# Hybrid decoder step: the norm row spread on TensorE, and two chunks put ahead of the sample

## The chip, the cores and the metric

One core of a Trainium2 chip runs the kernel. The metric is device microseconds of one execution, as the median of three runs. TensorE is PE, VectorE DVE, ScalarE ACT, GpSimd POOL, and SP the engine that does nothing but issue DMAs. Each engine works its own list of instructions strictly in order, and waits at the head of the list.

## The reference

The kernel is one inference step of two layers, a retention layer and a sliding-window attention layer, on 1024 prompt tokens and, with the same weights, on 8 sample tokens. All of it is float32, with 1024 features per token. What matters here is how the retention layer begins.

```python
def rmsnorm(x, g):
    xf = x.astype(jnp.float32)
    y = xf * lax.rsqrt(jnp.mean(xf * xf, axis=-1, keepdims=True) + EPS)
    return (y * g.astype(jnp.float32)).astype(x.dtype)

def retention_layer(x, S0, g_norm, w_in, g_out, w_out):
    h = rmsnorm(x, g_norm)
    proj = h @ w_in
    q, k, v, gate = jnp.split(proj, [RET_QK, 2 * RET_QK, 2 * RET_QK + RET_V], axis=-1)
    ...
    o, S = retention_scan(q, k, v, S0)
    ...
    return x + o @ w_out, S.astype(S0.dtype)
```

`g_norm` is one row of 1024 numbers, the norm row. The retention scan that follows the projections runs over chunks of 128 tokens and four heads.

## The kernel before

**Precision and products.** Every operand of a large product is split in two parts, a rounded one (`xh`, `woh`; `hi`, `w_hi`, on ACT) and the residual (`xl`, `wol`; `lo` on DVE, `w_lo` on POOL or DVE). A product is then three passes on PE: hi by hi, hi by lo, lo by hi. The weights of one head's q (set `q0`) come as four blocks A11, A12, A21, A22 of a 2x2 split, and the activations as blocks B11, B21 and so on.

**Chunks.** The prompt comes in as chunks c = 0 to 7 of 128 tokens (`X[c]`; tiles `xq`, `u`, one of `raw`) and the sample as c = 8, with 8 rows (a tile `u`). Each passes the same helpers: `xload` (SP issues its DMA), `sq` (ACT, L431: square and row sum), `pw` (POOL, L435 and L120: two small steps, the inverse root), `sc` (DVE, L440: scale the rows and multiply by `gb`), `TR` (PE, L105: eight transposes into two PSUM banks), `hi` (ACT, L457) and `lo` (DVE, L461). Their cores read:

```python
def sc(c):
    n = X[c].shape[0]
    dve.scalar_tensor_tensor(X[c], X[c], SS[c][:n], gb[:n], MUL, MUL)
def TR(c, b):
    PO[c] = [bank(b, j).rearrange("p (k t) -> p k t", k=4) for j in range(2)]
    for j in range(2):
        for k in range(4):
            tr(PO[c][j][:, k, :], X[c][:, 512 * j + k * 128:512 * j + k * 128 + 128], ident)
```

`gb` holds the norm row in all 128 partitions; a DMA writes it from the row, 512 KB in all. The sample takes another way after `sc`: eight transposes of 8 rows into a PSUM tile `pd8`, a copy into `rdec`, and `dcols` (DVE, L495 and L496), which writes two of its columns, rounded and as residual, behind the 256 prompt columns of B11 and B21. A first product of 258 columns (`plain`, L544) therefore needs chunks 0 and 2 and the sample, and A11 and A12.

**Order.** The order of an engine's list is the order in which the Python code calls the helpers. A hand-written opening takes chunks 8, 0 and 2 up to the first product; after it a table `ops` interleaves the helpers of the other chunks with the 16 first products, the next being chunk 1 (its transposes stand on PE behind two products).

**DMA semaphores.** All DMAs of SP and ACT take eight semaphores DMAHW0 to DMAHW7 in turn, and a DMA waits until the one that used its semaphore before has landed. So the semaphore that a DMA's row names in its wait is as a rule the one it raises itself.

**The ring of raw tiles and the memory under it.** `raw_tile()` (tag `raw`, five buffers of 4 KB per partition) hands out buffers in turn: first the raw weights of q0 and k0, then chunk 7, then all further weights. The last set of projections uses four of these tiles for its results as well; POOL scales them (L393) and SP spills them to DRAM, in eight DMAs `gsc<-raw` (L397). When the projections end, the pool is closed, and the scan's pools `rp0` and `rp` are laid over the same memory, with `reuse_waits="tile"`: the first writer of a new tile waits for whoever still uses the old tile under it.

```python
return wq.tile([128, 1024], F32, tag="raw", bufs=5, name="raw")
...
r = (raw_tile()[:, 0:516] if s is sets[-1] else ring(key)).rearrange("p (t n) -> p t n", t=2)
...
nc.sync.dma_start(out=M23, in_=a["c1"][:, 384:640])
```

In the scan a step loads q and k (`evp<-qks`, L735), v (`evx<-vsc`, L742) and the gate (`evc` or `evw<-gsc`, L748) on SP. DVE masks the scores (`sT`, L796), scales the finished output (`on`, L1067) and makes k's residual (`kl`, L791); ACT rounds the state (`Sh`, L1037) and `sT` (`sTh`, L801); PE transposes `on` (L105). M23, loaded at L1552, holds the masks of heads 2 and 3.

Of the kernel before, what the change touches and what calls it, by code (L numbers as in the profile page):

```python
# [7 lines left out]
F32 = mybir.dt.float32  # L8
# [6 lines left out]
D = 1024  # L15
# [45 lines left out]
def trunk(tc, x_prompt, x_sample, state_ret, cache_k, cache_v, norm_ret, w_in_ret, ret_out_norm,  # L61
          w_out_ret, norm_swa, w_in_swa, q_norm, k_norm, sinks, w_out_swa, c1, c2,
          y_p, y_s, nrp, nrs, nkp, nvp, nks, nvs):
    nc = tc.nc
    ctx = ExitStack()
    with ctx:
        ctx.enter_context(tc.manual_schedule(engines=MS))
        _trunk(ctx, tc, nc, locals())


def _trunk(ctx, tc, nc, a):
    x_prompt, x_sample, state_ret = a["x_prompt"], a["x_sample"], a["state_ret"]
    cache_k, cache_v = a["cache_k"], a["cache_v"]
    norm_ret, ret_out_norm, norm_swa = a["norm_ret"], a["ret_out_norm"], a["norm_swa"]
# [22 lines left out]
    mm = nc.tensor.matmul  # L97
# [6 lines left out]
    def tr(out, in_, ident, start=True, stop=True):  # L104
        nc.tensor.matmul(out, in_, ident, is_transpose=True, start=start, stop=stop)  # L105
# [13 lines left out]
    def rsq(out, in_, n):  # L119
        nc.gpsimd.tensor_tensor(out, in_, mhalf[:in_.shape[0], :n], ALU.pow)  # L120
# [13 lines left out]
    dcp = sa.enter_context(tc.tile_pool(name="dcp", bufs=1, reuse_waits="tile"))  # L134
    wq = sa.enter_context(tc.tile_pool(name="wq", bufs=1, reuse_waits="tile"))
# [26 lines left out]
    def bank(i, t):  # L162
        return abp.tile([128, 512], F32, tag=f"b{i}{t}", name=f"b{i}{t}")
# [7 lines left out]
    act, dve, pool = nc.scalar.activation, nc.vector, nc.gpsimd  # L171
# [21 lines left out]
    def src_of(s, name, sub):  # L193
        if name[0] == "A":
            return quad(s, int(name[1]) - 1, int(name[2]) - 1, sub)
        return s.sum[name, sub]
# [16 lines left out]
    def w_hi(s, name, sub):  # L213
        sh = [128, 512 // s.fw, s.fw]

        if (s.kind, s.h) == ("q", 0) and name in ("A11", "A12"):
            tag, n = ("s1", 2) if name == "A11" else ("s2", 2)
        else:
            tag, n = "wop", 12
        s.op[name, sub] = [wq.tile(sh, F32R, tag=tag, bufs=n, name=nm) for nm in ("woh", "wol")]  # L220
        act(s.op[name, sub][0], src_of(s, name, sub), AF.Copy)  # L221

    def w_lo(s, name, sub, eng=None):
        hi, lo = s.op[name, sub]
        eng = eng or (pool if name in ("A12", "A22") else dve)
        eng.tensor_tensor(lo, src_of(s, name, sub), hi.bitcast(F32), SUB)  # L226
# [183 lines left out]
    gb = sp.tile([128, D], F32, name="gb")  # L410
# [6 lines left out]
    def xload(c):  # L417
        if c in (0, 1, 2, 3):
            X[c] = xq.tile([128, D], F32, tag="xq", bufs=4, name="xq")
        elif c == 7:  # L420
            X[c] = raw_tile()
        else:
            X[c] = sp.tile([128, D], F32, tag="u", bufs=3, name="u")
        if c == 8:
            X[c] = X[c][0:ND, :]
        nc.sync.dma_start(out=X[c], in_=x_sample[:, 0, :] if c == 8 else x_prompt[0, c * 128:c * 128 + 128, :])

    def sq(c):
        SS[c] = sp.tile([128, 1], F32, name="ss", bufs=4)
        n = X[c].shape[0]  # L430
        act(junk[:n], X[c], AF.Square, accum_out=SS[c][:n])  # L431

    def pw(c):
        n = X[c].shape[0]
        pool.tensor_scalar(SS[c][:n], SS[c][:n], 1.0 / D, EPS, MUL, ADD)  # L435
        rsq(SS[c][:n], SS[c][:n], 1)
# [11 lines that stand above are left out]
# [4 lines left out]
    def where(c, j):  # L452
        return c // 4, ((B11, B21), (T3, B22))[c % 2][j], slice(128 * (c // 2 % 2), 128 * (c // 2 % 2) + 128)

    def hi(c, j):
        t, x, cs = where(c, j)
        act(XH[t][x][:, :, cs], PO[c][j], AF.Copy)  # L457

    def lo(c, j):
        t, x, cs = where(c, j)  # L460
        dve.tensor_tensor(XL[t][x][:, :, cs], PO[c][j], XH[t][x].bitcast(F32)[:, :, cs], SUB)  # L461
# [27 lines left out]
    def dcols(t, x, src=None):  # L489

        if src is None:
            k0, r0 = DB[x]
            src = rdec[:, k0:k0 + 4, r0 + 2 * t:r0 + 2 * t + 2]
        h = XH[t][x][:, :, 256:258]
        dve.tensor_copy(h, src)  # L495
        dve.tensor_tensor(XL[t][x][:, :, 256:258], src, h.bitcast(F32), SUB)  # L496
# [95 lines left out]
    q0, k0 = sets[0], sets[1]  # L592
# [270 lines left out]
    for r in range(2):  # L863
        pool.memset(oneh[:, r, r:r + 1], 1.0)
    pool.memset(rdec32, 0.0)
    nc.scalar.dma_start(out=gb, in_=norm_ret[0].partition_broadcast(128))
    nc.scalar.dma_start(out=ident, in_=a["c1"][:, 0:128])
    act(warm, warm, AF.Silu)
    for c in (0, 8, 2):
        xload(c)  # L870
# [5 lines left out]
        raw_load(k0, r, nc.sync)  # L876
    for c in (4, 6, 7):
        xload(c)
    for c in (8, 0, 2):
        sq(c)  # L880
        pw(c)
    sc(8)
    p8 = vdp.tile([128, 8, ND], F32, tag="vd", name="pd8")
    for k in range(8):
        tr(p8[:, k, :], X[8][:, k * 128:k * 128 + 128], ident[:ND, :ND])
    sc(0)
    TR(0, 1)
    dve.tensor_copy(rdec, p8)
    sc(2)
    TR(2, 2)  # L890
    dcols(0, B11)
    dcols(0, B21)
    for c, name in ((0, "A11"), (2, "A12")):
        for j in range(2):
            hi(c, j)
            lo(c, j)
        w_hi(q0, name, 0)
        w_lo(q0, name, 0, pool)
    ev.sort(key=lambda e: e[:2])
    for n, s in enumerate(slots):  # L900
        while pes and pes[0][0] <= s.t:
# [1348 lines left out]
    out = so_all()  # L2250
# [159 lines left out]
```

## Time and profile before

| | |
|---|---|
| median of three runs | 1292.86 us (1292.46 to 1294.36) |
| the profiled execution | 1292.86 us |
| its span, first to last instruction | 1291.0 us |
| mean granted TensorE clock | 0.997 |
| busy: PE, PEld, POOL, DVE, ACT | 98%, 94%, 55%, 60%, 51% |
| DMA, mean over the span | 160 GB/s |
| start of the first product | 15.76 us |

In the rows shown, the first number is the start in microseconds from the span's start, the second the duration; then the engine, the line, the operation and out<-in; xN is a count. In brackets stands the idle time of the engine just before, and what ended it. q1 is SP's DMA queue and q10 that of ACT; a row of a queue gives packets, megabytes and the share of the 16 DMA engines in the stretch asked for. A row of `windows` gives, after the stretch and its length, the busy time of PE, PEld, DVE, ACT and POOL with counts, the granted clock, the DMA share and GB/s.

### The profile page before, as it was taken

What the parts mean: (1) busy time and instruction counts of PE and PEld (TensorE: products, weight loads), DVE (VectorE), ACT (ScalarE), POOL (GpSimd) and SP (SyncE); (2) the same over time, 40 slices, a digit from 0 to 9 for tenths busy, and PEclk for the clock granted to TensorE, in tenths of its full rate; (3) what the DMA queues carried; (4) which work ended last, traced back from release to release, by engine and by line L of the source; (5) the groups of instructions that cost most, each with busy time, mean ns of one, the idle gap of its engine ahead of it and who ended that gap; (6) DMA issues with size and microseconds to landing.
All of it is one profiled execution on the core that took longest, in us unless ns stands there. A gap on an engine that the chain in (4) does not pass through costs nothing.

```text
span 1291.0 us, 26757 instructions
## 1 busy us (share of the span) xinstructions
PE 1266.2 (98%) x9839; PEld 1214.3 (94%) x9839; DVE 778.1 (60%) x1506; ACT 656.9 (51%) x1592; POOL 711.8 (55%) x822
## 2 busy tenths in 40 slices
PE   6999999999999999999999999999999999998998
PEld 5999999999999999888889999999999999998998
DVE  5954646665575764476774656764667766775421
ACT  5533445454555554578771235545566656663121
POOL 5654444535359899788771457726475655432000
PEclk9999999999999999999999999999999999998999
DMA  6313867687678673556879955843031222137232
GB/s 227 108 54 121 253 183 231 183 253 219 186 210 226 192 240 107 180 174 200 261 211 247 251 187 161 272 120 103 20 112 50 66 67 67 66 101 245 74 98 79
DMA packets 221967, 206.68 MB, mean 160 GB/s; under 512 B 32729, under 2 KB 196821, under 8 KB 221821
## 3 DMA queue, kind: packets, MB, share of 16 engines
q1 hardware_dynamic: 189840, 170.61, 44.2%
q10 hardware_dynamic: 31996, 34.36, 8.2%
q8 instruction: 78, 1.28, 0.4%
q14 instruction: 53, 0.43, 0.1%
HBM read 135.41 MB, written 70.55 MB: 160 GB/s over the span
## 4 chain that ended last, share of the span: by engine, by line
PE 90%; DVE 3%; DMA 2%; ACT 1%; POOL 1%; issue 1%; SPq 0%; ACTq 0%; POOLq 0%; DVEq 0%
PE S L1302 9%; PE b L335 8%; PE b L336 8%; PE b L337 8%; PE pj L1661 6%; PE pj L1662 5%; PE pj L1663 5%; PE b L328 4%; PE tr L105 4%; PE b L329 4%; PE b L330 4%; PE o L2023 2%; PE b L544 1%; PE S L335 1%; PE S L336 1%; PE S L337 1%
## 5 line engine op out<-in xcount | busy, mean ns | idle before, releaser
L335 PE MATMUL b<-xh,woh 128*128 128x258 f32 x784 | 223.2, 285 | 0.0
L337 PE MATMUL b<-xh,wol 128*128 128x258 f32 x784 | 221.7, 283 | 0.0
L336 PE MATMUL b<-xl,woh 128*128 128x258 f32 x784 | 221.6, 283 | 0.0
L1661 PE MATMUL pj<-SA,wh 128*128 128x384 f32 (+1 forms) x496 | 169.3, 341 | 4.5 <-ACT SA L2045 3.7
L1662 PE MATMUL pj<-SA,wh 128*128 128x384 f32 (+1 forms) x496 | 159.5, 322 | 0.7 <-DVE SA L2046 0.7
L1663 PE MATMUL pj<-SA,wl 128*128 128x384 f32 (+1 forms) x496 | 159.4, 321 | 0.0
L335 PEld LDWEIGHTS b<-xh,woh 128*128 128x128 f32 x784 | 148.0, 189 | 4.1 <-issue 3.7
L336 PEld LDWEIGHTS b<-xl,woh 128*128 128x128 f32 x784 | 148.7, 190 | 0.0
L337 PEld LDWEIGHTS b<-xh,wol 128*128 128x128 f32 x784 | 148.0, 189 | 0.0
L226 POOL TENSOR_TENSOR wol<-raw,woh 128x512 fp32r<-128x512 f32 x51 | 66.1, 1303 | 120.3 <-ACT woh L221 118.2
L328 PE MATMUL b<-woh,xh 128*128 128x256 f32 x448 | 126.6, 283 | 0.0
L329 PE MATMUL b<-wol,xh 128*128 128x256 f32 x448 | 126.0, 281 | 0.0
L330 PE MATMUL b<-woh,xl 128*128 128x256 f32 x448 | 125.6, 280 | 0.0
L2001 POOL TENSOR_TENSOR s<-s,sm 128x512 f32<-128x512 f32 x64 | 67.1, 1048 | 87.4 <-DVE sm L2000 76.4
L1661 PEld LDWEIGHTS pj<-SA,wh 128*128 128x128 f32 x496 | 93.9, 189 | 8.4 <-ACT SA L2045 4.0
L1662 PEld LDWEIGHTS pj<-SA,wh 128*128 128x128 f32 x496 | 94.3, 190 | 0.9 <-DVE SA L2046 0.9
L1663 PEld LDWEIGHTS pj<-SA,wl 128*128 128x128 f32 x496 | 93.9, 189 | 0.0
L1993 ACT ACTIVATE s<-s,mx 128x257 f32<-128x257 f32 x128 | 64.2, 503 | 48.9 <-DVE mx L1991 45.8
L328 PEld LDWEIGHTS b<-woh,xh 128*128 128x128 f32 x448 | 84.3, 188 | 5.0 <-issue 2.9
L330 PEld LDWEIGHTS b<-woh,xl 128*128 128x128 f32 x448 | 84.3, 188 | 0.0
L329 PEld LDWEIGHTS b<-wol,xh 128*128 128x128 f32 x448 | 84.3, 188 | 0.0
L221 ACT ACTIVATE woh<-s 128x512 fp32r<-128x512 f32 x88 | 54.1, 624 | 54.1 <-POOL s L211 20.7
(529 smaller groups left out, 3586.9 us busy)
## 6 DMA issues: line engine op xcount, KB each, us to landing
raw<-in_w_in_ret_dram ACTq DMA_DIRECT2D x44, 512.0 KB
st<-in_state_ret_dram SPq DMA_DIRECT2D x64, 256.0 KB
out_dram<-st SPq DMA_DIRECT2D x64, 256.0 KB
vb<-vscr SPq DMA_DIRECT2D x64, 128.0 KB
evp<-qks SPq DMA_DIRECT2D x32, 256.0 KB
evx<-vsc SPq DMA_DIRECT2D x32, 256.0 KB
wr<-in_w_in_swa_dram SPq DMA_DIRECT2D x32, 256.0 KB
evc<-gsc SPq DMA_DIRECT2D x16, 256.0 KB
```

The costliest lines, as they stand in the source:

```text
L226: eng.tensor_tensor(lo, src_of(s, name, sub), hi.bitcast(F32), SUB)
L328: mm(dst, xh, wh, start=a and i == 0, stop=False, skip_group_check=True)
L329: mm(dst, xh, wl, start=False, stop=False, skip_group_check=True)
L330: mm(dst, xl, wh, start=False, stop=z, skip_group_check=True)
L335: mm(dst, wh, xh, start=a, stop=False, **sg)
L336: mm(dst, wh, xl, start=False, stop=False, **sg)
L337: mm(dst, wl, xh, start=False, stop=z, **sg)
L1302: mm(box[0], s.op[f"A{i + 1}{j + 1}", 0][w][:, k, :], xs_[t][x[j]][:, k, :], start=(xs_ is XH and w == 0 and j + k == 0), stop=(xs_ is XL ...
L1661: mm(ps, hi[:, k, fs], xh[:, k, t0:t1], start=first and k == ks[0], stop=False)
L1662: mm(ps, hi[:, k, fs], xl[:, k, t0:t1], start=False, stop=False)
L1663: mm(ps, lo[:, k, fs], xh[:, k, t0:t1], start=False, stop=last and k == ks[-1])
L2001: nc.gpsimd.tensor_tensor(st[:, :, 0:256], st[:, :, 0:256], sm.unsqueeze(2).broadcast_to([128, 2, 256]), ALU.mult)
```

## The change

The norm row is loaded as one row of 4 KB, into a tile of the raw ring (`grow`). Two products of a row of ones (`row1`) with its halves spread it over the 128 partitions in PSUM, in the banks that the first product uses later, and two DVE copies bring it to `gb`. On every engine chunks 0 and 2 now come ahead of the sample, and DVE takes chunk 0's residuals before the sample's columns.

```diff
-    nc.scalar.dma_start(out=gb, in_=norm_ret[0].partition_broadcast(128))
+    grow = wq.tile([1, D], F32, tag="raw", bufs=5, name="raw")
+    nc.scalar.dma_start(out=grow, in_=norm_ret[0:1, :])
     nc.scalar.dma_start(out=ident, in_=a["c1"][:, 0:128])
+    row1 = dcp.tile([1, 128], F32, name="row1")
+    dve.memset(row1, 1.0)
     act(warm, warm, AF.Silu)
     for c in (0, 8, 2):
         xload(c)
     ...
     for c in (4, 6, 7):
         xload(c)
-    for c in (8, 0, 2):
+    bank_of = {}
+    for j in range(2):
+        bank_of[0, j] = bank(0, j)
+        mm(bank_of[0, j], row1, grow[:, 512 * j:512 * j + 512], start=True, stop=True)
+    for j in range(2):
+        dve.tensor_copy(gb[:, 512 * j:512 * j + 512], bank_of[0, j])
+    for c in (0, 2, 8):
         sq(c)
         pw(c)
+    sc(0)
+    TR(0, 1)
+    sc(2)
+    TR(2, 2)
     sc(8)
     p8 = vdp.tile([128, 8, ND], F32, tag="vd", name="pd8")
     for k in range(8):
         tr(p8[:, k, :], X[8][:, k * 128:k * 128 + 128], ident[:ND, :ND])
-    sc(0)
-    TR(0, 1)
+    for j in range(2):
+        hi(0, j)
+        lo(0, j)
+    w_hi(q0, "A11", 0)
+    for j in range(2):
+        hi(2, j)
     dve.tensor_copy(rdec, p8)
-    sc(2)
-    TR(2, 2)
     dcols(0, B11)
     dcols(0, B21)
-    for c, name in ((0, "A11"), (2, "A12")):
-        for j in range(2):
-            hi(c, j)
-            lo(c, j)
-        w_hi(q0, name, 0)
-        w_lo(q0, name, 0, pool)
+    for j in range(2):
+        lo(2, j)
+    w_lo(q0, "A11", 0, pool)
+    w_hi(q0, "A12", 0)
+    w_lo(q0, "A12", 0, pool)
```

DVE at the program's start, before; `b_184`, `b_185` are chunk 0's PSUM tiles, `b_196`, `b_197` chunk 2's, `pd_174` the sample's:

```order
L861 MEMSET warm 1x8
L440 SCALAR_TENSOR_TENSOR u<-u,ss,gb 8x1024
L440 SCALAR_TENSOR_TENSOR xq<-xq,ss,gb 128x1024
L888 COPY rdec<-pd_174 128x8x8
L440 SCALAR_TENSOR_TENSOR xq<-xq,ss,gb 128x1024
L495 CAST xh<-rdec 128x4x2
L496 TENSOR_TENSOR xl<-rdec,xh 128x4x2
L495 CAST xh<-rdec 128x4x2
L496 TENSOR_TENSOR xl<-rdec,xh 128x4x2
L461 TENSOR_TENSOR xl<-b_184,xh 128x4x128
```

The same place now; `b_164`, `b_166` hold the spread row, `b_183`, `b_184` are chunk 0's:

```order
L870 MEMSET row_137 1x128
L887 COPY gb<-b_164 128x512
L887 COPY gb<-b_166 128x512
L440 SCALAR_TENSOR_TENSOR xq<-xq,ss,gb 128x1024 x2
L440 SCALAR_TENSOR_TENSOR u<-u,ss,gb 8x1024
L461 TENSOR_TENSOR xl<-b_183,xh 128x4x128
L461 TENSOR_TENSOR xl<-b_184,xh 128x4x128
L905 COPY rdec<-pd_205 128x8x8
L495 CAST xh<-rdec 128x4x2
L496 TENSOR_TENSOR xl<-rdec,xh 128x4x2
```

The memset and two copies are new, the sample's scale (`u`) has gone behind both chunks', and its copy and casts behind chunk 0's residuals.

Further on, near 541 us, where the scan's tiles are first used, the order of the rows is the same as before, and their waits are not. SP, before, from the last three spills on:

```order
L397 DMA gsc<-raw 128x2x128 [waits DMAHW5_49,Pool_49]
L397 DMA gsc<-raw 128x2x128 [waits DMAHW6_49,Pool_49]
L397 DMA gsc<-raw 128x2x128 [waits DMAHW7_49,Pool_49]
L1552 DMA M_7448<-const_c_dram 128x256 [waits DMAHW0_49]
L742 DMA evx<-vsc 128x512 [waits DMAHW1_49,Activation_49]
```

The last two of these five now:

```order
L1566 DMA M_7457<-const_c_dram 128x256 [waits DMAHW5_49,DMAHW1_49,DMAHW0_49]
L742 DMA evx<-vsc 128x512 [waits Activation_49]
```

M23's load has gained the waits for DMAHW5 and DMAHW1, the first of the last three spills and the one before it, which are the two halves of one raw tile.

DVE there, before (`sT`, `on` and `kl` of one step):

```order
L796 TENSOR_TENSOR sT<-tr,M_89 128x128 [waits DMAHW1_49,PE_49]
L1067 TENSOR_SCALAR on<-po,ss 128x512 [waits Pool_49]
L791 SCALAR_TENSOR_TENSOR kl<-tr,M_89,kh 128x256 [waits Activation_49]
```

And now:

```order
L796 TENSOR_TENSOR sT<-tr,M_89 128x128 [waits DMAHW6_49,DMAHW7_49,PE_49,Pool_49]
L1081 TENSOR_SCALAR on<-po,ss 128x512 [waits PE_49,Pool_49]
L791 SCALAR_TENSOR_TENSOR kl<-tr,M_89,kh 128x256 [waits Activation_49]
```

`sT` waited for a weight load of long before (DMAHW1) and now waits for the second and third of the last three spills. On ACT the opposite happened: `Sh` waited for DMAHW1, DMAHW5 and two older spills, and now for one older spill (DMAHW0) alone, while `sTh` ahead of it waits, as `sT` does, for DMAHW6 and DMAHW7.

## The prediction

> **What bounds the kernel now.** I read the page's busy times and chain first, then the first 25 us instruction by instruction, then the DMA queues there, then the place near 541 us where the built program's waits differ.
>
> ```profile
> PE 1266.2 (98%) x9839; PEld 1214.3 (94%) x9839; DVE 778.1 (60%) x1506; ACT 656.9 (51%) x1592; POOL 711.8 (55%) x822
> PE 90%; DVE 3%; DMA 2%; ACT 1%; POOL 1%; issue 1%; SPq 0%; ACTq 0%; POOLq 0%; DVEq 0%
> ```
>
> PE is busy for 98% of the span and carries 90% of the chain: a microsecond is won only where PE waits. The change touches a time when PE has nothing to do yet. Timeline of that start (start, us, engine, line):
>
> ```profile
> 6.51 1.06 ACT L431 ACTIVATE junk<-u 8x1024 f32<-8x1024 f32 x1 [3.35 <-DMA u<-in_x_sample_dram]
> 7.69 1.06 ACT L431 ACTIVATE junk<-xq 128x1024 f32<-128x1024 f32 x1
> 8.60 1.27 DVE L440 SCALAR_TENSOR_TENSOR u<-u,ss,gb 8x1024 f32<-8x1024 f32 x1 [7.69 <-POOL ss L120]
> 8.93 1.00 POOL L435 TENSOR_SCALAR ss<-ss 128x1 f32<-128x1 f32 x1 [0.36 <-ACT junk L431]
> 9.92 1.01 PE L105 MATMUL pd<-ident,u 8*128 8x8 f32 x8 [9.92 <-DVE u L440]
> 10.01 0.56 POOL L120 TENSOR_TENSOR ss<-ss,mhalf 128x1 f32<-128x1 f32 x1
> 10.61 1.28 DVE L440 SCALAR_TENSOR_TENSOR xq<-xq,ss,gb 128x1024 f32<-128x1024 f32 x1 [0.74 <-POOL ss L120]
> 11.95 3.65 PE L105 MATMUL b<-ident,xq 128*128 128x128 f32 x16 [1.01 <-DVE xq L440]
> 12.62 1.28 DVE L440 SCALAR_TENSOR_TENSOR xq<-xq,ss,gb 128x1024 f32<-128x1024 f32 x1 [0.59 <-POOL ss L120]
> 14.39 2.65 DVE L461 TENSOR_TENSOR xl<-b,xh 128x512 fp32r<-128x512 f32 x4
> 15.76 0.75 PE L544 MATMUL b<-xh,woh 128*128 128x258 f32 x4 [0.17 <-ACT xh L457]
> 16.13 1.66 ACT L221 ACTIVATE woh<-raw 128x512 fp32r<-128x512 f32 x3
> 16.83 3.80 POOL L226 TENSOR_TENSOR wol<-raw,woh 128x512 fp32r<-128x512 f32 x3 [0.40 <-ACT woh L221]
> 20.98 0.54 POOL L120 TENSOR_TENSOR ss<-ss,mhalf 128x1 f32<-128x1 f32 x1
> 21.55 2.30 DVE L440 SCALAR_TENSOR_TENSOR xq<-xq,ss,gb 128x1024 f32<-128x1024 f32 x1 [3.33 <-POOL ss L120]
> 24.00 1.06 PE L105 MATMUL b<-ident,xq 128*128 128x128 f32 x8 [1.21 <-DVE xq L440]
> ```
>
> The chain to follow: sample landed (6.51), its square, scale and transposes; chunk 0 behind it (scale 10.61), chunk 2 (12.62), A12 rounded (16.13), three POOL residuals (16.83), chunk 1's scale (21.55), chunk 1's transposes on PE (24.00). From 24.00 on PE is nearly gapless, so what the change is worth at the start is how much earlier that last row comes.
>
> **The norm row.** The 512 KB broadcast goes, a 4 KB row comes. In the first rows of two DMA windows (2 to 2.5 us, and 2.5 to 5 us) and in SP's waits, q1 is SP's queue, q10 ACT's:
>
> ```profile
> q10 hardware_dynamic: 8, 0.03, 42.8%
> q1 hardware_dynamic: 101, 0.41, 50.9%
> q10 hardware_dynamic: 96, 0.39, 50.2%
> SPq L426 <- DMA gb<-in_norm_ret_dram: 2.5, 1, 2.5
> ```
>
> While chunk 0 comes in, the broadcast takes half of the engines. Alone, the same 0.41 MB of q1 take half of the 2.5 us. The sample, behind chunk 0 on that queue, then lands near 5.2 instead of 6.5; chunk 0, ahead of it, and with the shared stretch past 5.0 not counted yet, I put at 4.7 (range 4.4 to 5.4). Every later SP load comes about 1.3 us sooner; chunk 2, half a megabyte behind at the 0.8 MB that both queues moved in 2.5 us, at 6.2. SP's wait of 2.5 us for the broadcast's semaphore goes too; behind it stood chunk 3 and the next weights, while the loads issued before were streaming anyway.
>
> No row shows a 4 KB load at the start. ACT's first packets move between 2.0 and 2.5, so it cannot land before 2.4; later than chunk 0 at 4.7 it would be only if it were served behind it. I take 3.1, nearer the first, since nothing stands ahead of it on its queue.
>
> Two products of 1x128 by 1x512 are added on PE. The nearest row is the plain fp32 product of 512 columns:
>
> ```profile
> 76.76 1.92 PE L344 MATMUL vd<-raw,rdec 128*32 128x512 f32 x16
> L344 PE MATMUL vd<-raw,rdec 128*32 128x512 f32 x64 | 7.7, 598 | 0.0
> 26.82 1.13 PE L544 MATMUL b<-xl,woh 128*128 128x258 f32 x8
> L465 DVE COPY xq<-b 128x512 f32<-128x512 f32 x4 | 2.6, 680 | 0.0
> ```
>
> One lasts 0.60 us. The transposes at 11.95 take 3.65 for 16, at 24.00 1.06 for 8, half the pace, though the granted clock reads 1.00 in both windows; so early products cost double, some 1.0 us, and one starts 0.85 after the other. Products 3.2 to 5.1; each PSUM copy 0.68 (L465), so gb is whole near 5.8 (5.0 if PE runs at full pace).
>
> A rule that speaks against this: the Trainium skill, "FP8 and Floating Point Precision", section TensorE Precision Notes, says that true FP32 takes four passes through the array. The sixteen of L344, four column groups at a time, need 1.92 us in all, about 0.43 a round; an fp32r product of 258 columns needs 0.12 (eight in 1.13, less the last one's tail), so one pass over 512 is some 0.24 and a round is two passes, not four: the trace does not bear the rule out. By the rule gb would be whole near 7.6, and the sum below would end 0.8 us worse.
>
> **The order, chunk by chunk.** Chunk 0: square 4.7 to 5.9 (7.69 to 8.85 before, 1.16), POOL's two steps 0.19 and 0.56 to 6.8, scale at 6.8, gb ready by 1.0. Chunk 2: square from 6.2; its POOL step waits for the scale on DVE, as at 8.93, where 0.19 became 1.00; scale at 8.8 instead of 12.62. The sample's scale follows at 10.8. Transposes 8.1 to 11.8, rounding on ACT as before at the same distance: A12 at 12.3 (16.13). POOL's A11 residual now meets the sample's scale and waits until 12.1, so A12's starts at 13.4 instead of 16.83. Three times 1.27, chunk 1's two steps, its scale at 18.1 instead of 21.55: 3.4 us. The sample's tail is now last: sample scaled 12.1, two residuals of L461 in front of its copy, eight transposes (1.0), the copy and four small casts: first product at 13.8 instead of 15.76, only 2.0 sooner. From there to the end of two products it took 7.0 us (15.76 to 22.8) with 0.7 of stalls on A12 and residuals that go; PE gets to chunk 1's transposes at 20.2 to 20.8, its scale ends at 19.4 to 20.5. I take 20.6 for 24.00: **3.4 us won at the start**, between 2.2 (chunk 0 at 5.4, gb late) and 4.5.
>
> Edits at nothing, with the rows that hide them (SP's issue of chunk 7, the last of the loads, the squares of chunks 5 and 7):
>
> ```profile
> 10.53 0.43 SPq L426 DMA_DIRECT2D raw<-in_x_prompt_dram  x1
> 21.00:22.00 1.00, 1.00 (x11) 1.00 (x10) 0.45 (x1) 1.00 (x3) 1.00 (x2) 1.00 0.45 131
> 39.01 1.06 ACT L431 ACTIVATE junk<-u 128x1024 f32<-128x1024 f32 x1
> 42.99 1.07 ACT L431 ACTIVATE junk<-raw 128x1024 f32<-128x1024 f32 x1
> ```
>
> The ones' memset stands on DVE, idle until 8.60. Chunk 7's load now waits for the products, which have read its buffer by 5.1; it went out at 10.53. Chunk 5's, last on SP, waits for the sample's transposes (13.2); the loads ahead of it, which with it ended near 21.5, keep the DMA queue busy to about 18.7. Were these covers gone, the two chunks would come late by as much, and have 17 us until their squares.
>
> **What the diff does not show.** The norm row takes the first turn of the ring of raw tiles, so every later raw tile sits one buffer on. At 541 us new tiles are laid over that memory, and by the program's waits other tiles meet the last spills:
>
> ```profile
> 539.06 1.90 SPq L397 DMA_DIRECT2D gsc<-raw  x3
> 540.18 0.28 DVE L796 TENSOR_TENSOR sT<-tr,M 128x128 f32<-128x128 f32 x1
> 541.01 0.49 SPq L1552 DMA_DIRECT2D M<-const_c_dram  x1
> 541.39 0.75 DVE L1067 TENSOR_SCALAR on<-po,ss 128x512 f32<-128x512 f32 x1 [0.92 <-POOL ss L120]
> 542.19 0.65 PE L105 MATMUL tr<-ident,on 128*128 128x128 f32 x4 [0.18 <-DVE on L1067]
> 542.56 1.50 SPq L735 DMA_DIRECT2D evp<-qks  x2
> 543.16 1.09 ACT L1037 ACTIVATE Sh<-S 128x512 fp32r<-128x512 f32 x2 [1.58 <-DMA M<-const_c_dram]
> 548.45 0.68 PE L779 MATMUL tr<-evp 128*128 128x128 f32 x4 [0.97 <-DMA evp<-qks]
> DMA packets 338, 0.17 MB, mean 343 GB/s; under 512 B 18, under 2 KB 333, under 8 KB 338
> DMA packets 320, 0.16 MB, mean 319 GB/s; under 512 B 20, under 2 KB 317, under 8 KB 320
> ```
>
> The last two rows are the windows 541.5 to 542 and 542 to 542.5. Of the three spills (256 packets each) the first is through near 541.8 and lands by 543.16, where Sh, which waits for it in the program before, starts. The third is through near 542.65, so it lands near 544.0 (543.3 to 544.6). Now sT on DVE waits for the second and third: 544.0 instead of 540.18. Behind it on DVE stand `on` and kl; PE's transposes of `on` move from 542.19 to about 545.1, 2.9 us. Of this 0.97 is the wait that PE has anyway at 548.45: **1.9 us lost** (1.1 to 2.5). M's load on SP now waits for the first spill: 543.15 instead of 541.01, and evx, evw and evp behind it. The queue runs dry about 1.2 us, so evp lands near 549.5; PE asks for it at 550.3, so this is hidden behind the 1.9; with a shorter stall of sT it would be the bound, at 1.1.
>
> The Trainium skill, "DMA: Bandwidth & Descriptors", section Latency and other measured facts, calls HBM the slowest target and puts its receipt at up to 2 us under load. The first spill's 1.35 us agree; at 2 us the third would land at 544.6 and the loss be 2.5.
>
> **Sum.** -3.4 + 1.9 = -1.5 us. The profiled execution took 1292.86 us for a span of 1291.0, and is itself the median of the runs: 1292.86 - 1.5 = 1291.4. From no change only about 0.2%, 2.6 us, can be told here.
>
> **Rivals.**
> The stall at 541 costs nothing. For it: PE has slack of 0.97, and Sh already waited there for a spill. Against: `on` reached PE with no slack (0.18 idle at 542.19). Then 1292.86 - 3.4 = 1289.5.
> gb comes late (four passes, or the row landing past 4.7). Against: L344; for: no row of its kind. Start won 2.6, or 1.8: 1292.2, or 1293.0.
> The start gives little: the queue is slow until 2.5 with or without the broadcast, and the sample's tail holds PE. Won 2.0: 1292.8.
> Slower: SP's late M. If the six loads behind it stay 2.1 us late for several steps, and PE, which waits for evp already, pays this at two or three of them, 541 costs 6 us; it turns the sign from 3.4 on. For it: 5.75 us from evp's issue to PE's start. Against: at 548 the queue thins out (evc's load had long gone out). 1292.86 - 3.4 + 6 = 1295.5.
>
> **Chances.** Forecast 0.55, 541 free 0.19, gb late 0.12, little won 0.06, slower 0.08. The forecast's own range is 1289.8 to 1293.0 (won 2.2 to 4.5, lost 1.1 to 2.5, ends not all at once). With the free case and some of the late ones the range is 1288.9 to 1293.2. Faster by over 0.2% (under 1290.3): 0.17 of the free case and a fifth of the forecast, 0.28. Slower (over 1295.4): 0.05. Within: 0.67.
>
> **What would show it.** Chunk 0's scale near 6.8, the first product near 13.8, chunk 1's transposes near 20.6 with PE gapless behind them. Near 537 us sT standing behind a DMA for some 3 us, `on` and PE behind it, M's issue 2 us later than the third spill's. Wrong: gb's copies ending after 7; no wait of sT for a spill; PE waiting for evp longer than before.

## The result, and the profile after

The changed kernel is slower. Its median is 1297.5 us (1295.56 to 1297.78, 7 runs), that of the kernel before, run beside it, 1292.46 us (1290.8 to 1294.36, 7 runs). The ratio on record is 1.0029, with a 95% interval of 1.0019 to 1.0039; it is not the quotient of these two medians, which is 1.0039. So the change costs 3.7 us by the ratio and 5.0 us by the medians. A second comparison on another chip gave 1297.99 us and a ratio of 1.0044 (1.0032 to 1.0057). 1291.4 was predicted, and 1293.2 was the top of the range.

The profiled execution took 1296.3 us for a span of 1294.5, 3.5 us more than the profile before. Two lines of its page, busy time and the engines' shares of the chain:

```profile
PE 1274.0 (98%) x9843; PEld 1219.5 (94%) x9843; DVE 783.4 (61%) x1509; ACT 656.7 (51%) x1592; POOL 711.2 (55%) x822
PE 91%; DVE 2%; DMA 2%; POOL 2%; ACT 1%; issue 1%; SPq 0%; ACTq 0%; POOLq 0%; DVEq 0%
```

PE's busy time has risen by 7.8 us, twice what the two new products take (3.75), so PE is not just waiting: some of its work runs slower. The timeline of the start shows where. Lines of the code behind the change lie 14 further down than before.

```profile
2.44 3.75 PE L885 MATMUL b<-raw,row 1*128 1x512 f32 x4 [2.44 <-DMA raw<-in_norm_ret_dram]
6.22 0.69 DVE L887 COPY gb<-b 128x512 f32<-128x512 f32 x1 [1.01 <-PE b L885]
7.14 1.28 DVE L440 SCALAR_TENSOR_TENSOR xq<-xq,ss,gb 128x1024 f32<-128x1024 f32 x1 [0.22 <-DVE gb L887]
9.15 1.28 DVE L440 SCALAR_TENSOR_TENSOR xq<-xq,ss,gb 128x1024 f32<-128x1024 f32 x1 [0.73 <-POOL ss L120]
11.13 1.27 DVE L440 SCALAR_TENSOR_TENSOR u<-u,ss,gb 8x1024 f32<-8x1024 f32 x1 [0.69 <-POOL ss L120]
11.68 5.75 POOL L226 TENSOR_TENSOR wol<-raw,woh 128x512 fp32r<-128x512 f32 x4 [0.58 <-ACT woh L221]
12.46 1.02 PE L105 MATMUL pd<-ident,u 8*128 8x8 f32 x8
13.78 1.21 DVE L495 CAST xh<-rdec 128x8 fp32r<-128x8 f32 x1
15.02 1.20 DVE L496 TENSOR_TENSOR xl<-rdec,xh 128x8 fp32r<-128x8 f32 x1
15.13 2.51 PE L544 MATMUL b<-xh,woh 128*128 128x258 f32 x8 [1.66 <-DVE xh L495]
16.34 1.12 DVE L496 TENSOR_TENSOR xl<-rdec,xh 128x8 fp32r<-128x8 f32 x1
17.44 1.93 PE L544 MATMUL b<-xh,wol 128*128 128x258 f32 x8
20.88 1.43 PE L544 MATMUL b<-xh,woh 128*128 128x258 f32 x8
22.15 1.12 PE L544 MATMUL b<-xh,wol 128*128 128x258 f32 x8
24.07 1.04 PE L105 MATMUL b<-ident,xq 128*128 128x128 f32 x8
```

The same casts before, and POOL's first residual there:

```profile
13.82 0.17 DVE L495 CAST xh<-rdec 128x8 fp32r<-128x8 f32 x1
15.14 1.28 POOL L226 TENSOR_TENSOR wol<-raw,woh 128x512 fp32r<-128x512 f32 x1 [2.56 <-ACT woh L221]
```

The reader is to see three things. Chunk 0 and chunk 2 are scaled at 7.14 and 9.15, 3.5 us before their old places, and the sample, now the last of the three, at 11.13, 1.5 us before the last scale of before. Three of the sample's four small casts (the two L495, which round, and the two L496, which take the residual) take 1.1 to 1.2 us each, where before they took 0.17; all the while POOL works on its residuals (11.68 to 17.43), which before began at 15.14, behind the casts. And the first product waits 1.66 us for the first cast and then runs at half pace: eight of its instructions take 1.93 us from 17.44 on, against 1.12 from 22.15 on (the 2.51 at 15.13 hold a short wait for the next cast as well). Full pace comes at 21.6. So chunk 1's transposes come at 24.07, and before they came at 24.00. Nothing is left of the start.

Near 541 us, the timeline of SP, DVE and PE (their rows one after the other):

```profile
540.52 1.48 SPq L397 DMA_DIRECT2D gsc<-raw  x3
543.74 0.35 SPq L1566 DMA_DIRECT2D M<-const_c_dram  x1
544.53 0.29 DVE L796 TENSOR_TENSOR sT<-tr,M 128x128 f32<-128x128 f32 x1 [1.79 <-DMA gsc<-raw]
544.74 0.74 DVE L1081 TENSOR_SCALAR on<-po,ss 128x512 f32<-128x512 f32 x1
545.53 0.66 PE L105 MATMUL tr<-ident,on 128*128 128x128 f32 x4 [3.09 <-DVE on L1081]
```

Here the stall stands as it was foreseen: `sT` behind the spills, PE's transposes at 545.53 instead of 542.19, idle 3.09 us ahead of them.

One more loss was not foreseen. Two stretches of 3.4 us, by windows (us; busy time of PE, PEld, DVE, ACT, POOL with counts; granted clock; DMA share; GB/s):

```profile
970.46:973.88 3.42, 2.54 (x19) 2.12 (x19) 1.64 (x4) 3.12 (x7) 3.36 (x3) 1.00 0.11 20
973.88:977.29 3.41, 3.41 (x12) 3.41 (x11) 2.92 (x8) 1.56 (x5) 1.93 (x4) 0.50 0.72 251
```

For one window of 3.41 us PE was granted half its clock, after a stretch in which it had idled for a quarter of the time. That costs 1.7 us here (the table below, from 2.15 at 860 to 3.85 at 980). The profile before has such windows only from 1179 to 1186, behind a wait of PE of 3.7 us; all profiles here show half pace at that place.

How far a profile is ahead of the one before (-) or behind it (+) can be read at any place: the starts of the same ACT, DVE and POOL instructions, counted from the program's end, are subtracted, and the median of a few us is taken. Each row is one execution: the two of the changed kernel differ by 1.8 us at 560, the two of e5's kernel by 0.6 at 50 and 1.6 at the end. For all kernels of this study:

| us behind before at | 50 | 530 | 560 | 860 | 980 | 1160 | end |
|---|---|---|---|---|---|---|---|
| changed kernel | -0.18 | 0.46 | 2.15 | 2.15 | 3.85 | 3.85 | 3.50 |
| the same, second profile | 0.01 | 0.01 | 3.94 | 4.35 | 4.30 | 4.31 | 3.60 |
| e8_turnonly | -1.11 | -0.70 | 2.70 | 2.91 | 2.79 | 2.80 | 1.83 |
| e2_turn | 0.37 | 0.37 | 3.29 | 3.35 | 3.30 | 3.31 | 3.01 |
| e9_shift | 0.33 | 0.33 | 0.73 | 0.72 | 0.63 | 0.63 | 0.78 |
| e1_ring | -0.50 | -0.01 | -0.38 | 0.73 | 1.15 | 1.15 | 1.61 |
| e3_fill | -1.01 | -1.01 | -1.71 | -1.28 | -0.95 | -0.94 | -1.42 |
| e4_row | -1.33 | -1.27 | -1.57 | -1.59 | -1.55 | -1.54 | -1.41 |
| e7_pw | -1.89 | -1.56 | -2.26 | -2.26 | -1.83 | -1.82 | -1.53 |
| e5_psum | -2.88 | -2.85 | -2.92 | -2.67 | -0.74 | -0.74 | -0.82 |
| e5_again | -2.25 | -1.83 | -1.86 | -1.61 | -1.65 | -1.64 | -2.41 |
| e6_both | -3.33 | -3.27 | -2.82 | -2.13 | 0.21 | 0.23 | -0.71 |
| e6_again | -3.16 | -2.09 | -2.55 | -1.95 | 1.57 | 1.58 | 0.93 |
| f1_small | -1.70 | 0.02 | -0.58 | 0.21 | 4.38 | 4.38 | 3.98 |
| f2_twice | 0.55 | 0.61 | -0.58 | 1.90 | 2.15 | 2.15 | -0.57 |

### The profile page after: what moved, and what is told of

It reads as the page before. It is cut to its first block, busy times and chain, and to the rows that moved or that the text cites. A ratio compares the mean times of both kernels' runs of the same rounds, so it can differ in the third digit from the quotient of the medians.

```text
span 1294.5 us, 26768 instructions
## 1 busy us (share of the span) xinstructions
PE 1274.0 (98%) x9843; PEld 1219.5 (94%) x9843; DVE 783.4 (61%) x1509; ACT 656.7 (51%) x1592; POOL 711.2 (55%) x822
## 3 DMA queue, kind: packets, MB, share of 16 engines
q8 instruction: 78, 1.28, 0.4%
## 4 chain that ended last, share of the span: by engine, by line
PE 91%; DVE 2%; DMA 2%; POOL 2%; ACT 1%; issue 1%; SPq 0%; ACTq 0%; POOLq 0%; DVEq 0%
PE S L1316 9%; PE b L335 8%; PE b L337 7%; PE b L336 7%; PE pj L1675 6%; PE pj L1676 6%; PE pj L1677 6%; PE b L328 4%; PE tr L105 4%; PE b L329 4%; PE b L330 4%; PE b L544 3%; PE o L2037 2%; PE S L335 1%; PE S L336 1%; PE S L337 1%
```

## The experiments

Times are medians, each with its ratio to the kernel before run on the same chip, and the 95% interval of the ratio. One thousandth is 1.3 us. Some expectations call the place near 541 us, where the scan's pools take over the memory, the seam.

### The place near 541 us

**e1_ring.** The changed kernel, its row and its ones without tiles of their own:

```diff
-    grow = wq.tile([1, D], F32, tag="raw", bufs=5, name="raw")
+    grow = gb[0:1, :]
-    row1 = dcp.tile([1, 128], F32, name="row1")
+    row1 = gs[0:1, 0:128]
```

> The changed kernel with the norm row loaded into the first row of gb itself and the ones kept in an existing tile, so the ring of raw tiles and every address are as before the change; the start is that of the changed kernel. Theory A (two causes: the seam at 541 us costs 2.1 to 2.3 us because of the ring, and the start wins nothing because PE runs its first two products at half pace): near 540 us sT waits for no spill again and the offset against before stays where the start left it, -1 to +1 us; in all 2 us less than the changed kernel, 1292 to 1295.5. Rival B (the seam is not what counts; the loss lies in the second half, at 966 to 977 us): the time stays near 1297.

Measured: 1293.12 us, 1.0001 (0.9992 to 1.001). DVE and PE in the timeline:

```profile
540.17 0.28 DVE L796 TENSOR_TENSOR sT<-tr,M 128x128 f32<-128x128 f32 x1
542.19 0.66 PE L105 MATMUL tr<-ident,on 128*128 128x128 f32 x4 [0.19 <-DVE on L1081]
```

The stall is gone, and by the interval the time is that of before. So the loss of the changed kernel hangs on where the row and the ones lie.

**e2_turn.** The kernel before, with one turn of the ring more:

```diff
+    turn = raw_tile()
+    dve.memset(turn[0:1, 0:8], 0.0)
     nc.scalar.dma_start(out=gb, in_=norm_ret[0].partition_broadcast(128))
```

> The kernel before with one unused turn of the ring of raw tiles at its start (eight numbers are set to zero in it) and nothing else changed. Theory A: the start is as before to 0.1 us, the first sT of the scan waits for the spills until about 544.5 instead of 540.2, the transposes of `on` come 3.3 us later and 2.1 to 2.3 us are left behind 550 us: 1294.5 to 1295. Rival B: the stall is there, and is absorbed further on: 1292.5.

Measured: 1295.89 us, 1.0021 (1.0012 to 1.003). A timeline row, and in a second fence a row of windows:

```profile
544.10 0.29 DVE L796 TENSOR_TENSOR sT<-tr,M 128x128 f32<-128x128 f32 x1 [3.48 <-DMA gsc<-raw]
```

```profile
545.44:548.86 3.42, 3.42 (x14) 3.03 (x13) 2.42 (x6) 2.68 (x9) 1.68 (x4) 0.50 0.59 192
```

The stall came, and after it a window at half pace; the median is 0.9 us above the range expected. SP's load of M was not late here (541.38), and yet the loss from 530 to 560 is 2.9 us: M's lateness is not needed for it.

**e8_turnonly.** The changed kernel with `row1 = gs[0:1, 0:128]` alone, so the ring's turn stays.

> The changed kernel with only the ones row moved into an existing tile, so that no address is shifted by its 512 bytes; the norm row still takes a turn of the raw ring. Theory H (the ring alone makes the loss at 541): sT, M and the transposes of `on` stand behind the spills as in the changed kernel, 1.7 to 2.3 us are left behind 550 us, or 3.5 to 4 where a window of half pace follows the stall, and the time is that of the changed kernel, 3 to 5.5 us above before. Rival I (the shift of all addresses by 512 bytes makes part of it): 1 us or more below the changed kernel.

Measured: 1296.04 us, 1.0025 (1.0015 to 1.0035). Windows at the start and behind the stall, then `sT`:

```profile
12.01:15.42 3.41, 1.32 (x14) 1.02 (x13) 3.34 (x6) 3.41 (x6) 3.41 (x3) 1.00 1.09 373
15.42:18.84 3.42, 3.09 (x15) 2.81 (x15) 3.39 (x6) 0.21 (x2) 2.76 (x4) 0.50 1.02 405
...
544.49:547.90 3.41, 3.34 (x13) 3.15 (x14) 2.59 (x7) 2.44 (x7) 1.24 (x3) 0.50 0.90 281
```

```profile
543.55 0.29 DVE L796 TENSOR_TENSOR sT<-tr,M 128x128 f32<-128x128 f32 x1 [4.01 <-DMA gsc<-raw]
```

**e9_shift.** The kernel before with `row1` added and set, and not used.

> The kernel before with nothing but the ones row added, a tile of 512 bytes that is set once and not used: all addresses behind it move by 512 bytes. Theory H: nothing changes, within 0.8 us of before. Rival I: 1 us or more slower.

Measured: 1293.32 us, 1.0006 (0.9997 to 1.0015). `sT` waits for no spill:

```profile
542.55 0.28 DVE L796 TENSOR_TENSOR sT<-tr,M 128x128 f32<-128x128 f32 x1
```

So the ring's turn makes the wait for the spills and most of the loss. What the shift costs is 0.8 us by its ratio, with an interval that takes in zero. It isn't without effect, though: in all three profiles in which the ones have a tile of their own (the changed kernel twice, and this one) the `Sh` of the step before starts behind an idle time of ACT of 1.9 us that `po` on PE ends (539.51 here), and in all thirteen others behind 0.7 us that `S` ends. Here that alone puts `sT` at 542.55 instead of 540.18 and PE's transposes of `on` at 544.12 instead of 542.19, of which 0.4 us is left at 560. In the changed kernel this delay runs beside the wait for the spills, so that the two don't add up: DVE idles 1.79 us ahead of `sT` there, and 4.01 in e8_turnonly. Whether e8_turnonly (+3.2 us by its ratio) is really below the changed kernel (+3.7 and +5.7), the intervals don't tell.

**after_again.** The changed kernel itself.

> The changed kernel once more, for a second profile beside the runs of this chip. If the half pace of one clock step at 973 us and the wait at 386 us belong to this execution alone and not to the kernel, the second profile shows them elsewhere or not at all, while the stall at 541 us (2.1 to 2.3 us) is there again; median 1295 to 1297.5.

Measured: 1297.99 us, 1.0044 (1.0032 to 1.0057). A row of DVE, then a window:

```profile
544.78 0.29 DVE L796 TENSOR_TENSOR sT<-tr,M 128x128 f32<-128x128 f32 x1 [2.47 <-DMA gsc<-raw]
```

```profile
547.12:550.53 3.41, 3.41 (x10) 2.66 (x9) 2.71 (x7) 2.23 (x7) 1.96 (x3) 0.50 0.93 323
```

The median is 0.5 us above the range expected. The window at 973 is gone, as expected of a chance event, and a window at half pace stands behind the stall instead. Of the four profiles with the turned ring three show it there, and none of the twelve others shows one there. From 530 to 560 us the four lose 1.7, 3.9, 3.4 and 2.9 us, the first without that window.

### The start

**e3_fill.** e1_ring with `fill(n)`, n transposes of the identity into an unused bank: 10 ahead of `sc(0)`, 9 behind `TR(2, 2)`, 14 behind the sample's.

> As e1_ring, with 33 transposes of the identity into an unused PSUM bank put between PE's own work at the start: 10 ahead of chunk 0's transposes, 9 behind chunk 2's, 14 behind the sample's; they keep PE busy and compute nothing that is used. Theory A (the half pace of the first products ate the gain of the start): PE reaches full pace before the first product, chunk 1's transposes come near 21 instead of 24.07, and 2.5 to 3 us are won against e1_ring, 1290 to 1292. Rival C (the start is bound by DVE and POOL, not by PE's pace): chunk 1's transposes come earlier but the work at 31.8 us (t34 of chunk 1 on POOL) does not, and the time is that of e1_ring. Rival D: the fillers come in the way, and the first product starts later than 15.13.

Measured: 1293.25 us, 1.0001 (0.9992 to 1.001), and the expectation was missed. PE reached full pace at 9.84, and then:

```profile
17.57 0.71 PE L544 MATMUL b<-xh,woh 128*128 128x258 f32 x4 [1.73 <-DVE xh L495]
...
22.93 1.03 PE L105 MATMUL b<-ident,xq 128*128 128x128 f32 x8
```

At full pace PE simply waits in the middle of its first product for the cast of B21. The pace alone gives 0.5 us over e1_ring (the table at 50), no more than two profiles of one kernel differ by; the casts are the bound underneath.

**e5_psum.** e1_ring, with the casts reading the sample's transposes in PSUM:

```diff
-    dcols(0, B11)
-    dcols(0, B21)
+    dcols(0, B11, p8[:, 0:4, 0:2])
+    dcols(0, B21, p8[:, 4:8, 0:2])
```

> As e1_ring (changed order and row, ring as before), with the sample's four small casts on DVE reading the sample's transposes in PSUM instead of their copy in SBUF. Theory F (a small DVE cast between two SBUF tiles waits while POOL writes a residual: 1.21, 1.20 and 1.12 us instead of 0.17 in the changed kernel, though L461 on DVE, which reads PSUM, is not held up there): the four take some 0.7 us together instead of 3.7, the first product starts near 14.1 instead of 15.13; whether chunk 1's transposes then come at 20.5 or at 23 is set by when PE comes to full pace. 0 to 3 us won against e1_ring, 1290 to 1293. Rival G (they are slow because the tiles are fp32r, or as operations of 8 columns): still 1.2 each from PSUM, and the time is that of e1_ring.

Measured: 1291.16 us, 0.9989 (0.998 to 0.9998). DVE and PE:

```profile
13.48 0.15 DVE L495 CAST xh<-pd 128x8 fp32r<-128x8 f32 x1
13.66 0.17 DVE L496 TENSOR_TENSOR xl<-pd,xh 128x8 fp32r<-128x8 f32 x1
13.75 0.16 DVE L495 CAST xh<-pd 128x8 fp32r<-128x8 f32 x1
13.94 0.17 DVE L496 TENSOR_TENSOR xl<-pd,xh 128x8 fp32r<-128x8 f32 x1
...
13.78 2.06 PE L544 MATMUL b<-xh,woh 128*128 128x258 f32 x8 [0.48 <-DVE xh L495]
...
21.07 1.03 PE L105 MATMUL b<-ident,xq 128*128 128x128 f32 x8
```

POOL is as busy as before (11.50 to 17.28), the tiles written are the same fp32r tiles with the same 8 columns, and the four casts take 0.15 to 0.17. What held them up was the SBUF source while POOL ran: shown. The first product starts at 13.78 and chunk 1's transposes at 21.07, 2.9 us earlier than before and 2.4 earlier than in e1_ring (23.49).

The Trainium skill, "SBUF — State Buffer", section SBUF: two separate sides, has this as a rule: DVE and GpSimd share a pair of ports, taken as an exclusive lock for a whole instruction, by a DVE operation with two SBUF inputs or in a two-port mode. The trace agrees, 1.21 against 0.15 us; that a cast with one SBUF input runs in such a mode, no row here shows.

**e5_again.** The same kernel.

> e5_psum once more on another chip, for its time: 1.0 to 1.5 us below before if the first comparison (0.9989) holds, and chunk 1's transposes again near 21.1.

Measured: 1290.63 us, 0.998 (0.9971 to 0.999), the fastest version of this study: 2.6 us below before by its ratio, more than expected, and below before in both comparisons. Chunk 1's transposes came at 21.72.

**e4_row.** The kernel before in its old order, with the small row in `gb[0:1, :]`, the two products and the copies.

> The kernel before in its old order (the sample first), with only the norm row changed: 4 KB into gb's first row, two products with ones, two copies; ring and addresses as before. Theory A: gb is whole near 6.9, so the sample's scale comes at about 7.3 instead of 8.60 and the first product about 1 us earlier than 15.76; what is left of it behind 24 us depends on when PE comes to full pace, 0 to 1.2 us won, 1291.3 to 1292.5. Rival E (the small load and the products themselves cost the time, not the order): slower than before by 1 us or more.

Measured: 1291.87 us, 0.9994 (0.9985 to 1.0003): no difference from before by the time; 1.3 us ahead in the profile from 50 us to the end. The sample's scale and chunk 1's transposes:

```profile
7.27 1.27 DVE L440 SCALAR_TENSOR_TENSOR u<-u,ss,gb 8x1024 f32<-8x1024 f32 x1 [0.22 <-ACT junk L431]
```

```profile
22.66 1.06 PE L105 MATMUL b<-ident,xq 128*128 128x128 f32 x8 [1.23 <-DVE xq L440]
```

The row and its products do no harm, so rival E falls. In the old order the casts come before POOL's residuals, and take 0.17 each.

**e7_pw.** e4_row with chunk 1's POOL steps ahead of A22's residual.

```diff
-         o(w_lo, q0, "A22", 0), o(xload, 5), o(sq, 1), o(pw, 1)],
+         o(sq, 1), o(pw, 1), o(w_lo, q0, "A22", 0), o(xload, 5)],
```

> As e4_row (old order, small row), with chunk 1's two small POOL steps put ahead of POOL's residual of A22. In e4_row PE waited 1.23 us for chunk 1's scale, which waited for POOL. Expected: chunk 1's transposes at 21.4 to 21.8 instead of 22.66, 0.8 to 1.2 us less than e4_row, 1290.5 to 1291. Rival: A22's residual, now later, stops the second product by as much, and the time is that of e4_row.

Measured: 1292.17 us, 0.9995 (0.9986 to 1.0004). Chunk 1's transposes come at 21.40, as expected, and only 0.6 us of that is left at 50 us; the time shows nothing. Inconclusive.

### Whether a gain at the start reaches the end

**e6_both.** e5_psum with the fillers (10, 9 and 6).

> As e5_psum, with the idle PE filled as in e3_fill by transposes into an unused bank (10, 9 and 6 of them). Theory: PE at full pace from about 9.8, the casts not in the way, the first product at 14.1 without a stop inside, chunk 1's transposes at 20 to 21, 3 us earlier than before's 24.00; ring as before, so nothing is lost at 541: 1289.5 to 1290.5 where before gives 1293. If the pace and the casts were not what ate the start's gain: 1292 to 1293, as e1_ring.

Measured: 1293.78 us, 1.0011 (1.0002 to 1.0021). The start does what was expected:

```profile
13.97 1.19 PE L544 MATMUL b<-xh,woh 128*128 128x258 f32 x8
...
20.57 1.09 PE L105 MATMUL b<-ident,xq 128*128 128x128 f32 x8 [0.56 <-DVE xq L440]
```

It is 3.3 us ahead until 530 us, and yet its median is above that of before. **e6_again** is the same kernel.

> e6_both once more on another chip. Its profile was 3.3 us ahead of before behind the start, yet its runs were 1.4 us slower than before. If that is a property of the kernel (the fillers cost something later, or being early costs it), it is slower than e5 again by 1.5 us or more; if it belonged to that chip or that loading, it is at or below e5, 1290 to 1291.

Measured: 1294.3 us, 1.0014 (1.0002 to 1.0025): a property of the kernel. Of the 3.3 us e6_both loses 2.3 between 860 and 980 (e6_again 3.5, with a half-pace window at 895). There the chain of waits shows weight loads that end late, of e6_both first, of e5_psum below (start, us):

```profile
887.02 4.71 DMA wr<-in_w_in_swa_dram
949.13 4.12 DMA wr<-in_w_in_swa_dram
957.58 4.09 DMA wr<-in_w_in_swa_dram
```

```profile
886.49 3.26 DMA wr<-in_w_in_swa_dram
944.51 3.86 DMA wr<-in_w_in_swa_dram
955.39 3.16 DMA wr<-in_w_in_swa_dram
```

These rows show the late loads, and not the 2.6 us between the two medians: the two profiled executions are nearly as long as one another (1292.08 and 1291.98 us), since that of e5_psum, the slowest of its eleven runs, loses 1.9 us in the same stretch to a half-pace window at 969.

**f1_small** has 23 transposes of 8 columns in place of the fillers (16 ahead of `sc(0)`, 3 ahead of `sc(2)`, 4 behind the sample's), **f2_twice** e6's fillers as twice as many of 64 columns.

> As e5_psum, with 23 transposes of 8 columns in PE's idle time at the start (16 ahead of chunk 0's, 3 ahead of chunk 2's, 4 behind the sample's), which is about as many instructions on PE as e6_both's 25 fillers. Theory J (what e6 loses later comes from the number of PE's instructions: its program is fetched by DMA in pieces, and a piece that is read at another moment meets the weight loads that PE waits for near 887 and 949 us): as in e6 the piece falls near 889 instead of 895 to 898, the load of wr lands about 1.4 us later there, and the time is 2 us or more above e5_psum, 1293 to 1294. Theory K (e6 loses because it is early, or for its full-width fillers): as e5_psum, 1290.5 to 1291.5.

> As e6_both, with each filler of 128 columns replaced by two of 64: about the same time on PE, twice as many instructions. Theory J: the piece moves on by as much again, to about 883, ahead of the load that PE waits for at 887, and the loss there is gone: start 3.2 us ahead of before and most of it kept, 1290 to 1291. Theory K: as e6_both, 1293.5 to 1294.5.

Measured: f1_small 1294.85 us, 1.0014 (1.0004 to 1.0024); f2_twice 1292.14 us, 0.9996 (0.9985 to 1.0008). The chain in f1_small, and in f2_twice:

```profile
889.36 4.87 DMA wr<-in_w_in_swa_dram
951.81 3.99 DMA wr<-in_w_in_swa_dram
960.26 4.04 DMA wr<-in_w_in_swa_dram
```

```profile
890.47 3.18 DMA wr<-in_w_in_swa_dram
959.83 3.14 DMA wr<-in_w_in_swa_dram
```

f1_small has e6's late loads although it is 2.3 us later than e6 there and does almost no extra work on PE, so being early is not the cause. Nearly the same work in twice as many instructions (f2_twice) has no late loads in its chain. That speaks for the number of PE's instructions. The DMA records show the reads of the program itself, in pieces of 16 KB that take 0.9 to 1.4 us: one starts at 897.6 before, at 895.2 in e5_psum, at 889.2 in e6_both and at 891.7 in f1_small, in the last two inside the load that PE waits for, and at 888.8 in f2_twice, ahead of it. But e3_fill, with a piece at 888.2 inside its load of 887.29, lost nothing (3.46 us). So theory J is likely and not shown. f2_twice tests this place only: its fillers came in the way, and its first product started at 16.97; its piece moved less than expected (888.8, not 883), and its median lies between what the two theories gave.

## Why the prediction was wrong, step by step

**Seen rightly.** Chunk 0, chunk 2 and the sample were scaled at 7.14, 9.15 and 11.13 (6.8, 8.8 and 10.8 predicted). Nothing showed that the ones' memset or the loads of chunks 5 and 7 cost anything. At 541 the mechanism held row for row: `sT` at 544.53 (544.0), the transposes of `on` at 545.53 (545.1), M at 543.74 (543.15), and PE did not wait for evp afterwards. None of the prediction's three signs of being wrong came: gb's copies ended at 6.9, under the 7 that it named.

**The products.** The row landed by 2.44 (3.1 predicted), and the two products took 3.75 us, not 1.9, so `gb` was whole at 6.9 (5.8); the scales are late by the 0.3 us that follow. The rule that was weighed against the trace (the Trainium skill, "FP8 and Floating Point Precision", section TensorE Precision Notes: four passes for true FP32) was right, and my reading of L344 wrong. At half pace an fp32r product of 258 columns takes 0.215 (eight from 17.44 to 19.16), so one pass over 512 takes 0.43, and four passes 1.7 us, a little under half of the 3.75. The two products have four records, two each, so L344's sixteen records were eight products: two rounds of four passes of 0.24, which are its 1.92 us.

**The step that failed: "the copy and four small casts: first product at 13.8".** The casts were put down at about the 0.17 us that they took before, where POOL happened to be idle (12.58 to 15.14). The new order puts them among POOL's residuals, and three took 1.1 to 1.2 us; the first product came at 15.13 and chunk 1's transposes at 24.07, not 20.6. With them out of the way the first product starts at 13.78 and chunk 1's transposes at 21.07 or 21.72 (e5_psum), with PE at full pace as well at 20.57 or 20.28 (e6): 13.8 and 20.6 had been predicted. That 13.8 is met so closely is in part luck, as the scales ahead of it were 0.3 late. Of the 3.4 us, 2.3 to 2.9 were there once the casts were out of the way, and 3.2 to 3.3 with full pace as well (the table at 50); the times of e5's kernel show 1.4 and 2.6 us. The casts, and the pace that hangs on them, ate it.

**Within it, the pace.** "It took 7.0 us with 0.7 of stalls that go" took PE's pace over from before. It took 8.9 us, since the cast left PE idle 1.66 us ahead of the product, and PE came to full pace at 21.6 instead of 15.1. In e8_turnonly the clock had been granted at 12.0, and was halved for the window behind that gap. By itself this is the smaller part, some 0.5 us (e3_fill against e1_ring).

**The mis-sized term: "1.9 us lost".** The four profiles with the turned ring lose 1.7 to 3.9 us there, 3.0 in the mean. What was left out is that a stall of 3 us on PE can be followed by 3.4 us at half pace. By times, e2_turn loses 2.7 us (1.6 to 3.9) and e8_turnonly 3.2 (1.9 to 4.5).

**The sum as it was:** about 0 at the start and +3.0 at 541, and then what comes by chance in one execution or another: half-pace windows (973 here, 969 in e5_psum, 974 in f1_small), a late weight load at 386 (0.6 us by the table). The two comparisons give +3.7 and +5.7 us. e1_ring against the changed kernel says that the place of the row and the ones is nearly all of it, and e2_turn and e8_turnonly that the ring's turn is most of it; whether anything beyond 3 us is systematic stays open.

**The rivals.** The one on the slower side, 1295.5, came nearest, and for the wrong reason: SP's late M was not what PE waited for, and e2_turn has the loss without it. "541 free" falls. "gb late" had the four passes right, but with the row there 0.7 us sooner than assumed it cost the scales 0.3 us and no more. "The start gives little" happened, to a gain of nothing where it put 2.0: not for a slow queue, but in the sample's tail, whose casts POOL held up.

**The chances.** 0.05 for slower was far too low. The start's gain and the stall at 541 were two estimates that I let err by their rows' spread, and both errors, the casts and the clock, came from what an operation shares with its neighbours, which no row of the old order could show.

## What to carry to other kernels

A duration belongs to the company in which it was measured: before a small DVE operation between SBUF tiles is moved, look at what POOL does at its new place, and let it read PSUM if it can. A tile that takes a turn of a ring moves every later tile of that ring, and the bill may come where another pool is laid over the same memory, 500 us on; a scratch row belongs in a tile that is there already. A wait of PE costs its length and, at times, a window of 3.4 us at half pace behind it.

## What the runs showed of the hardware

The half pace comes and goes on a grid of 3.41 us: by the changes of the clock that the trace records, every half-pace window inside a span is 3.41 or 6.83 us long, and in the changed kernel the full pace from 21.56 to 973.88 lasted 952.32 us, 279 times 3.413. The same program can meet the grid at another phase: e5's kernel came to full pace at 17.0 in one profile and at 18.1 in the other, though its first product began only 0.3 us later. PE came to full pace at 15.1, 15.8 and 16.4 in the profiles of the old order with the old broadcast; in the changed order, without fillers and with the casts held up, at 20.1, 21.5 and 21.6, and in e8_turnonly at 12.0 and, after a window at half pace, again at 18.8. The Trainium skill, "TensorE: Matmul & The Clock Gate", section What's actually happening, describes such a free-running window of 3413 ns, and the trace agrees; how much idle time in a window halves the clock the runs don't settle, since in the changed kernel it followed on 2.54 us busy of 3.42 at 970, and did not follow on 1.68 of 3.41 from 543.80 to 547.21, another window of the same grid. At the start of a span, where no change of the clock has been recorded yet, the granted clock reads 1.00 at half pace: there the pace has to be read from the products.
